# Third convolution part by seven products, the first head's scores ahead of z, and a shorter norm chain, in a hybrid encoder block

## The chip, the cores and the metric

The kernel runs on one core of a Trainium2 chip. The metric is the device time in microseconds (us) of one execution. The engines are named as in the profile: PE multiplies matrices (PEld loads its weights beside it), DVE works on vectors, ACT computes activations, POOL does small operations and issues DMAs through its own queue, SP issues DMAs.

## The reference

One layer over 512 tokens of width 1024, in float32:

```python
h = rmsnorm(x, g_mix)
xc, gb, gc, q, k, v, g_sw, gate_a, gate_r = split(h @ w_in)   # widths 1024 x5, 2048 x2, 1024 x2
u = gc * xc
conv = centred 3-tap convolution of u along the tokens
y_a = (gb * conv) @ w_a_out
ret = retention(rotary(q), rotary(k), v), forward with and backward without the diagonal; 4 heads
ret = per-head normalisation of ret, times g_ret
y_r = (ret * silu(g_sw)) @ w_r_out
x = x + (sigmoid(gate_a) * y_a + sigmoid(gate_r) * y_r) @ w_o
x = x + (silu(rmsnorm(x, g_ffn) @ w_ff_gate) * (rmsnorm(x, g_ffn) @ w_ff_up)) @ w_ff_down   # 2816 wide
return rmsnorm(x, g_final)
```

## The kernel before

**Precision.** Each operand is split in two, a rounded high part (`hi`, a cast on ACT, L203) and the rest (`lo`, a subtract on DVE, L204), and each product is three matmuls: high by high, high by low, low by high (`mm3`, L342 to L344, and the inner loops of `prod`, L383, and `prod_tm`, L427).

**Seven products for eight.** Most large products are done on a grid of 2 x 2 blocks with seven block products, by the Strassen-Winograd scheme. For that, sums of weight quarters are needed (`FORMS`: b11, t1, t2, b21, t3, t4, b22) and sums of activations (`s1` to `s4`). A sum of weights is made in one of two ways: on DVE from two loaded quarters (L301), or, for the sets listed in `SUMMED`, in DRAM by DMAs that add (`sum_step`), so that the kernel loads it ready-made. `strassen` (tokens on the partitions) and `fm_quad` (features on the partitions) run the seven products.

**Order of the weights.** `PLAN` lists every weight unit in the order of use; `take` hands out the next and starts casting and splitting those after it, and `load_raws` and `prefetch_block` issue their loads on SP's queue. There are ten raw tiles (512 KB each) and five pairs of split tiles. A list scheduler at compile time orders the instructions of each engine: the order of the program is the priority, and work that it expects to be ready earlier may go ahead. `tc.issue_after(ins)` puts what the block issues on the engine of `ins` behind it.

**Stages.** First q and k of three heads, then six weight sets of seven products each for v with the swish gate and for the two branch gates (`do_quad`). Their results go to DRAM by POOL's queue (`store`). Behind some of these stores stands a `sum_step`, at up to three places of each `do_quad`; they make the sums for the first two feed-forward sets.

Then the convolution branch. Its 1024 features go in four parts of 256. x and C of parts 0 and 1 are two sets of seven products and B of both is one more (`mix_quads`); their results are split and stored as forms of z (`z_forms`, 16 stores on POOL for both). Then follow head 0's loads, its scores (`do_scores`) and the splitting of its v (`split_v`). Part 2 goes through `do_mix(2)`, with eight block products each for x, C and B (`feature_major`, a block of 48 matmuls). Then for each head: loads of the next head's q, k, v and gate, the value product (`do_pv`), the next head's scores, a transpose (`do_t`), and either part 3 of the convolution (`do_mix(3)`) or the output product of the head before.

After the merge comes the product with `w_o`. While its last products run, each block of 128 tokens (`nb`) is normed for the feed-forward: `join` adds the product to x, `complete` stores it, squares it with a running sum (L1031), adds the two halves' sums (L1035, on ACT), raises to the power -1/2 on POOL (L1036) and scales both halves on DVE (L1039); `tr_o` transposes the result on PE (L1053), splits it and copies it. `first_tokens` runs the first feed-forward products between the transposes.

The feed-forward goes in parts of 3, 4 and 4 sets. The down product of a part (`down`) adds its result into a DRAM copy of x (`ydr`) by accumulating DMAs on POOL (`add_y`); the last part reads that copy.

Of the kernel before, what the change touches and what calls it, by code (L numbers as in the profile page):

```python
# [17 lines left out]
P = 128  # L18
D = 1024
# [49 lines left out]


def plan():

# [73 lines left out]

SUMMED = (("f", 0), ("f", 1), ("o",))

# [23 lines left out]
def block_kernel(ctx: ExitStack, tc: tile.TileContext, xw0, xw, xT, xtok, wpack, wquad, cols, decs, rot, g_ffn, g_final, out):  # L172
# [49 lines left out]
    block = [0]  # L222

    made = []
    ready = []
# [6 lines left out]
    def prefetch_block(loads, splits):  # L232
        i = block[0]
        block[0] += 1
        st = [rawtile(), rawtile()]
        units = []
        for c in range(2):
            if loads:
                loads(c)
            nc.sync.dma_start(st[c], wpack[i][:, c * QH:(c + 1) * QH])  # L240
        for c in range(2):
            hi, lo = unit()
            units.append((hi, lo))
            split(st[c], hi, lo)
            if splits:
                splits(c)
        return units
# [14 lines left out]

    steps = {"quads": sums_of(SUMMED[:2]), "heads": sums_of(SUMMED[2:])}

# [14 lines left out]
    loaded = [0]  # L279

    def load_raws(upto):
        while loaded[0] < len(LOADS) and LOADS[loaded[0]][0] <= upto:
            _, quad, name, u, n = LOADS[loaded[0]]
            t = rawtile()
            src = wsum[quad, name, u] if name[0] == "t" else quarter(quad, name, u)
            nc.sync.dma_start(t[:, 0:n], src[:, 0:n])
            raws[quad, name, u] = t
            loaded[0] += 1

# [499 lines left out]
    def z_forms(s, z):  # L789
# [3 lines left out]
        def put(j, t):  # L793
            n = t.shape[1]
            hl = [t512(F32R)[:, 0:256 * n].rearrange("p (f t) -> p f t", f=n) for _ in range(2)]
            split(t, *hl)
            for d, x in zip(zd[j], hl):
                store(d[:, :, s, :], x.bitcast(F32))
        v, w = (t512().rearrange("p (f t) -> p f t", f=2) for _ in range(2))
# [5 lines left out]
        put(2, w)  # L805
        put(3, x2[:, 1:2])

    def do_mix(s):
        us, c = [], bigtile()[:, 0:2, :]
        feature_major(xg, lambda m, ps: us.append(snap(ps)))  # L810
        u = u_tile()

        def ev_c(m, ps):
            nc.vector.tensor_tensor(out=u[:, m, 1:513], in0=ps, in1=us[m], op=ALU.mult)
            conv(m, 2 * s + m, u[:, m], c[:, m])
        feature_major(xg, ev_c)

        def ev_b(m, ps):
            nc.vector.tensor_tensor(out=c[:, m], in0=ps, in1=c[:, m], op=ALU.mult)
        feature_major(xg, ev_b)  # L820
        z_forms(s, c)

    T1, T2 = slice(0, 256), slice(256, 512)

    def halves(t):
        return t.rearrange("p (m t) -> p m t", m=2)

    def mix_quads():

        c = bigtile().rearrange("p (s m) t -> p s m t", s=2)  # L830
        for s in range(2):
            u, got = u_tile(), {}

            def ev21(ps):
                nc.vector.tensor_tensor(out=u[:, :, 257:513], in0=halves(ps), in1=halves(got["c2"]), op=ALU.mult)

            def ev12(t):
                nc.vector.tensor_tensor(out=u[:, :, 1:257], in0=halves(got["x1"]), in1=halves(t), op=ALU.mult)
            fm_quad(xf, lambda t: got.update(x1=t), ev21, lambda t: got.update(c2=t), ev12)
            for m in range(2):  # L840
                conv(m, 2 * s + m, u[:, m], c[:, s, m])
# [7 lines left out]
        for s in range(2):  # L849
            z_forms(s, c[:, s])  # L850


    def load(src, dt=F32):
        t = bigtile(dt)
        nc.sync.dma_start(t if dt == F32 else t.bitcast(F32), src)
        return t

    def load_head(h):
        tab = misctile(896, "tab")
        nc.sync.dma_start(tab, tabs[h])  # L860
        return [load(t, F32R) for t in qkd[h]], tab, load(vd[h]), load(sgd[h])

# [165 lines left out]
    def complete(nb, half, last):  # L1028
# [3 lines left out]
        if not last:  # L1032
            nc.gpsimd.tensor_scalar_add(ac[:, 3:4], ac[:, 0:1], EPS)
            return
        nc.scalar.activation(ac[:, 4:5], ac[:, 1:2], AF.Identity, bias=ac[:, 3:4])  # L1035
        nc.gpsimd.tensor_tensor(out=ac[:, 5:6], in0=ac[:, 4:5], in1=mhalf[:, 0:1], op=ALU.pow)  # L1036
# [65 lines left out]

    def ev(tt):
        if tt == 0:
            tr_o(1)
        join(2 + tt, 0, a[tt])
        complete(2 + tt, 0, 1)
# [5 lines left out]
    act = {}  # L1113
    gates = {}

    def act_tiles(names):
# [6 lines left out]
    def gated(q, th, g, u):  # L1123
# [5 lines left out]
        if not gates.get(q0):  # L1129
# [3 lines left out]
                               for j in range(2))  # L1133
        s = t512()
        nc.scalar.activation(s, g, AF.Silu)
        nc.vector.tensor_tensor(out=s, in0=u, in1=s, op=ALU.mult)
# [71 lines left out]
    def down(n):  # L1208
        strassen(n, act_forms(), lambda tt, t: add_y(t, tt, 0), lambda tt, ps: add_y(snap(ps), 2 + tt, 0),
                 lambda tt, t: add_y(t, 2 + tt, 1), lambda tt, t: add_y(t, tt, 1))  # L1210

# [194 lines left out]
```

## Time and profile before

| | |
|---|---|
| median of three runs | 1022.86 us (1022.56 to 1025.2) |
| profiled execution | 1025.12 us |
| span in that execution, first to last instruction | 1023.3 us |
| mean granted clock of PE | 0.997 |
| busy PE / DVE / ACT / POOL | 1014.1 / 903.1 / 550.0 / 137.0 us |

The times of one execution hang together; the profiled one lies 2.26 us above the median of the others. A row of a timeline reads: start, duration, engine, line, operation, output <- inputs, shape, count, and in brackets the idle time ahead of it and what ended that. A row of the waits reads: engine and line that waited, what it waited for, us in total, times, the longest. SPq, POOLq and ACTq are DMAs issued by that engine.

### The profile page before, as it was taken

What the parts mean: (1) busy time and instruction counts of PE and PEld (TensorE: products, weight loads), DVE (VectorE), ACT (ScalarE), POOL (GpSimd) and SP (SyncE); (2) the same over time, 40 slices, a digit from 0 to 9 for tenths busy, and PEclk for the clock granted to TensorE, in tenths of its full rate; (3) what the DMA queues carried; (4) which work ended last, traced back from release to release, by engine and by line L of the source; (5) the groups of instructions that cost most, each with busy time, mean ns of one, the idle gap of its engine ahead of it and who ended that gap; (6) DMA issues with size and microseconds to landing.
All of it is one profiled execution on the core that took longest, in us unless ns stands there. A gap on an engine that the chain in (4) does not pass through costs nothing.

```text
span 1023.3 us, 14820 instructions
## 1 busy us (share of the span) xinstructions
PE 1014.1 (99%) x5586; PEld 884.6 (86%) x5586; DVE 903.1 (88%) x1161; ACT 550.0 (54%) x748; POOL 137.0 (13%) x225
## 2 busy tenths in 40 slices
PE   9999999999999999999999999999999999999997
PEld 7888888888888998888888888879998999899986
DVE  7877998979798988797989998999998999889996
ACT  7556655553656455343543335586654565556554
POOL 0020221222112003202122100020002000110011
PEclk9999999999999999999999999999999999999999
DMA  9525487694766657848597855473318522663533
GB/s 351 191 86 187 166 297 216 212 315 151 256 204 227 256 198 267 326 146 331 125 342 294 292 181 165 162 268 96 125 41 224 178 84 83 190 161 104 166 68 98
DMA packets 53352, 200.24 MB, mean 196 GB/s; under 512 B 7264, under 2 KB 7392, under 8 KB 48672
## 3 DMA queue, kind: packets, MB, share of 16 engines
q1 hardware_dynamic: 37600, 137.39, 38.8%
q0 software_dynamic: 15392, 61.62, 20.7%
q8 instruction: 44, 0.72, 0.3%
q10 hardware_dynamic: 288, 0.29, 0.1%
q14 instruction: 28, 0.23, 0.1%
HBM read 160.73 MB, written 55.31 MB: 211 GB/s over the span
## 4 chain that ended last, share of the span: by engine, by line
PE 93%; DVE 4%; issue 1%; ACT 1%; DMA 0%; POOL 0%; POOLq 0%; DVEq 0%; ACTq 0%
PE bank L427 35%; PE bank L383 28%; PE bank L342 10%; PE bank L344 10%; PE bank L343 10%; DVE wlo L204 1%; DVE xform L204 1%; DVE big L1026 1%; PE bank L477 0%; DMA ydr<-big 0%; DVE big L1006 0%; PE bank L662 0%; DVE big L980 0%; PE bank L1053 0%; DVE big L979 0%
## 5 line engine op out<-in xcount | busy, mean ns | idle before, releaser
L203 ACT CAST whi<-raw 128x1024 fp32r<-128x1024 f32 (+2 forms) x299 | 303.1, 1028 | 268.4 <-PE bank L427 64.7
L204 DVE TENSOR_TENSOR wlo<-raw,whi 128x1024 fp32r<-128x1024 f32 (+2 forms) x300 | 353.1, 1193 | 70.6 <-ACT whi L203 70.1
L383 PE MATMUL bank<-xform,whi 128*128 128x256 f32 x1424 | 258.8, 284 | 0.0
L383 PEld LDWEIGHTS bank<-xform,whi 128*128 128x128 f32 x1424 | 223.4, 193 | 0.9 <-ACT t L434 0.5
L383 PE MATMUL bank<-xform,wlo 128*128 128x256 f32 x712 | 201.6, 284 | 0.0
L427 PE MATMUL bank<-whi,big 128*128 128x512 f32 x596 | 187.6, 390 | 0.0
L427 PE MATMUL bank<-whi,xform 128*128 128x512 f32 x496 | 157.1, 390 | 0.0
L301 DVE TENSOR_TENSOR raw<-raw 128x1024 f32<-128x1024 f32 (+1 forms) x128 | 151.8, 1204 | 3.6 <-DMA raw<-wquad 2.7
L383 PEld LDWEIGHTS bank<-xform,wlo 128*128 128x128 f32 x712 | 137.1, 193 | 0.0
L427 PEld LDWEIGHTS bank<-whi,big 128*128 128x128 f32 x596 | 111.8, 188 | 24.2 <-ACT t L434 0.4
L427 PE MATMUL bank<-wlo,big 128*128 128x512 f32 x298 | 116.0, 389 | 0.0
L427 PEld LDWEIGHTS bank<-whi,xform 128*128 128x128 f32 x496 | 93.0, 188 | 19.6 <-DVE xform L204 0.4
L427 PE MATMUL bank<-wlo,xform 128*128 128x512 f32 x248 | 96.5, 389 | 0.0
L434 ACT COPY t<-bank 128x512 f32<-128x512 f32 x105 | 61.2, 586 | 56.0 <-PE bank L383 29.7
L342 PE MATMUL bank<-big,whi 128*128 128x512 f32 x220 | 85.7, 390 | 0.0
L344 PE MATMUL bank<-big,wlo 128*128 128x512 f32 x220 | 85.6, 389 | 0.0
L343 PE MATMUL bank<-big,whi 128*128 128x512 f32 x220 | 85.6, 389 | 0.0
L427 PEld LDWEIGHTS bank<-wlo,big 128*128 128x128 f32 x298 | 56.0, 188 | 11.4
L427 PEld LDWEIGHTS bank<-wlo,xform 128*128 128x128 f32 x248 | 46.6, 188 | 9.5
L342 PE MATMUL bank<-whi,big 128*128 128x512 f32 x128 | 49.8, 389 | 0.0
L343 PE MATMUL bank<-wlo,big 128*128 128x512 f32 x128 | 49.8, 389 | 0.0
L344 PE MATMUL bank<-whi,big 128*128 128x512 f32 x128 | 49.8, 389 | 0.0
(200 smaller groups left out, 1372.5 us busy)
## 6 DMA issues: line engine op xcount, KB each, us to landing
raw<-wquad SPq DMA_DIRECT2D x140, 512.0 KB, 4.6
raw<-wpack SPq DMA_DIRECT2D x42, 512.0 KB, 5.8
t_f<-wquad POOLq DMA_DIRECT2D x12, 512.0 KB, 6.9
z<-t POOLq DMA_DIRECT2D x24, 256.0 KB, 4.6
t_o<-wquad POOLq DMA_DIRECT2D x12, 512.0 KB, 6.9
zform<-z POOLq DMA_DIRECT2D x6, 1024.0 KB, 7.7
v<-t POOLq DMA_DIRECT2D x16, 256.0 KB, 5.2
sg<-t POOLq DMA_DIRECT2D x16, 256.0 KB, 4.8
```

Source lines behind the costliest of these rows:

```text
L203: first = (round or nc.scalar.copy)(hi, src)
L204: low_of[0] = nc.vector.tensor_tensor(out=lo, in0=src, in1=hi.bitcast(F32), op=ALU.subtract)
L301: nc.vector.tensor_tensor(out=t, in0=t, in1=raws[quad, more, u][:, 0:n], op=ALU.add)
L342: nc.tensor.matmul(ps, lh, rh, start=first, stop=False)
L343: nc.tensor.matmul(ps, lh, rl, start=False, stop=False)
L344: nc.tensor.matmul(ps, ll, rh, start=False, stop=last)
L383: nc.tensor.matmul(o, l[:, c], r[:, k], start=start and s == 0 and k == 0 and i == 0, stop=stop and k == 3 and i == 2, skip_group_check=True)
L427: nc.tensor.matmul(pss[tt], l, r[:, c], start=start and k == 0 and i == 0, stop=stop and k == n - 1 and i == 2, skip_group_check=True)
L434: nc.scalar.copy(t, ps)
L1026: nc.vector.tensor_tensor(out=yt, in0=yt, in1=ps, op=op)
```

## The change

Four things are changed.

1. **Third part.** x and C of part 2 of the convolution become a set of seven products (`XC`), behind those of parts 0 and 1 and ahead of B of parts 0 and 1. Its weight sums are made in DRAM: it stands first in `SUMMED`, and `do_quad` gets one more place for a `sum_step` (four for three). `do_mix(2)` keeps B alone.
2. **Order.** Head 0's q, k, v and gate are loaded among the weight loads of the second and third sets. Its v is split and its scores run ahead of `z_forms` of parts 0 and 1 (`put_z`). Head 1's q and k are loaded on POOL's queue behind the last store of z. Weight blocks that follow are loaded on SP behind head 0's loads.
3. **Norm.** The add of the two sums (L1035) goes from ACT to POOL, and for token block 2 the `join` stands ahead of `tr_o(1)`.
4. **First down part.** It is stored to a tensor of its own (`first`) by plain DMAs. Eight accumulating DMAs from DRAM to DRAM add it to `ydr`, behind a small POOL operation that reads the gate of the first set of the second part.

```diff
+XC = ("x", C_XC + 512, C_GC + 512)
-    for c0, c1 in ((C_XC, C_GC), (C_XC + 256, C_GC + 256), (C_GB, C_GB + 256)):
+    for c0, c1 in ((C_XC, C_GC), (C_XC + 256, C_GC + 256), XC[1:], (C_GB, C_GB + 256)):
...
-        for c in (C_XC, C_GC, C_GB):
+        for c in (C_GB,) if s == 2 else (C_XC, C_GC, C_GB):
...
-SUMMED = (("f", 0), ("f", 1), ("o",))
+SUMMED = (XC, ("f", 0), ("f", 1), ("o",))
...
-            nc.sync.dma_start(st[c], wpack[i][:, c * QH:(c + 1) * QH])
+            with tc.issue_after(behind[-1].ins) if behind else nullcontext():
+                nc.sync.dma_start(st[c], wpack[i][:, c * QH:(c + 1) * QH])
...
-    steps = {"quads": sums_of(SUMMED[:2]), "heads": sums_of(SUMMED[2:])}
+    steps = {"quads": sums_of(SUMMED[:1]) + sums_of(SUMMED[1:3]), "heads": sums_of(SUMMED[3:])}
...
+            if among and loaded[0] % 3 == 0:
+                with tc.issue_after(raw.ins):
+                    among.pop(0)()
...
-                if tt and not o:
+                if tt:
                     sum_step(last)
...
+    def xc_quad(s, c):
+        u, got = u_tile(), {}
+        def ev21(ps):
+            nc.vector.tensor_tensor(out=u[:, :, 257:513], in0=halves(ps), in1=halves(got["c2"]), op=ALU.mult)
+        def ev12(t):
+            nc.vector.tensor_tensor(out=u[:, :, 1:257], in0=halves(got["x1"]), in1=halves(t), op=ALU.mult)
+        fm_quad(xf, lambda t: got.update(x1=t), ev21, lambda t: got.update(c2=t), ev12)
+        for m in range(2):
+            conv(m, 2 * s + m, u[:, m], c[:, m])
+    def put_z():
+        for s in range(2):
+            stored = z_forms(s, made_z[0][:, s])
+        with tc.issue_after(stored.ins):
+            second.extend(load(t, F32R, nc.gpsimd) for t in qkd[1])
...
+        xc_quad(0, c[:, 0])
+        head = []
+        for src, dt in ((qkd[0][0], F32R), (qkd[0][1], F32R), (vd[0], F32), (sgd[0], F32)):
+            among.append(lambda src=src, dt=dt: head.append(load(src, dt)))
+        xc_quad(1, c[:, 1])
+        part2.append(bigtile()[:, 0:2, :])
+        xc_quad(2, part2[0])
...
-        for s in range(2):
-            z_forms(s, c[:, s])
+        while among:
+            among.pop(0)()
+        tab = misctile(896, "tab")
+        nc.sync.dma_start(tab, tabs[0])
+        made_z.append(c)
+        behind.append(last[3])
+        return head[0:2], tab, *head[2:]
...
     def do_mix(s):
+        if s == 2:
+            c = part2[0]
+        else:
             ... x and C by two blocks, as before
...
-    mix_quads()
-    nxt = load_head(0)
+    nxt = mix_quads()
+    vv, sg = split_v(nxt[2]), nxt[3]
     p = do_scores(nxt[0], nxt[1])
-    vv, sg = split_v(nxt[2]), nxt[3]
+    put_z()
     do_mix(2)
...
-            nxt = load_head(h + 1)
+            nxt = load_head(h + 1, second if h == 0 else None)
...
-        nc.scalar.activation(ac[:, 4:5], ac[:, 1:2], AF.Identity, bias=ac[:, 3:4])
+        nc.gpsimd.tensor_tensor(out=ac[:, 4:5], in0=ac[:, 1:2], in1=ac[:, 3:4], op=ALU.add)
...
+        join(2 + tt, 0, a[tt])
         if tt == 0:
             tr_o(1)
-        join(2 + tt, 0, a[tt])
         complete(2 + tt, 0, 1)
...
+    first = dram.tile([S, D], F32, name="first_part")
+    def put_first(t, nb, half):
+        nc.gpsimd.dma_start(first[nb * P:(nb + 1) * P, half * 512:(half + 1) * 512], t)
+    def add_first(behind):
+        with tc.issue_after(behind.ins):
+            for nb in range(NB):
+                for half in range(2):
+                    add_y(first[nb * P:(nb + 1) * P, half * 512:(half + 1) * 512], nb, half)
...
             pair(q)
+            if q == q_add:
+                mark = small.tile([P, 1], F32, tag="mark", name="mark", bufs=1)
+                add_first(nc.gpsimd.tensor_scalar_add(mark, gate_of[0][:, 0:1], 0.0))
         if q0 + n < NQ:
-            down(n)
+            down(n, add_y if q0 else put_first)
```

More of the change, by code (lines that the diff above doesn't have):

```diff
@@ L1 @@
-from contextlib import ExitStack
+from contextlib import ExitStack, nullcontext
 import numpy as np
@@ L222, in block_kernel @@
     block = [0]
+    behind = []
     made = []
@@ L279, in block_kernel @@
     loaded = [0]
+    among = []
     def load_raws(upto):
@@ L797, in put @@
             for d, x in zip(zd[j], hl):
-                store(d[:, :, s, :], x.bitcast(F32))
+                stored = store(d[:, :, s, :], x.bitcast(F32))
+            return stored
         v, w = (t512().rearrange("p (f t) -> p f t", f=2) for _ in range(2))
@@ L805, in z_forms @@
         put(2, w)
[L806 to L821, printed above, removed]
+        return put(3, x2[:, 1:2])
     T1, T2 = slice(0, 256), slice(256, 512)
@@ L826, in halves @@
         return t.rearrange("p (m t) -> p m t", m=2)
+    def xc_quad(s, c):
[7 more added lines that the diff above has]
+            conv(m, 2 * s + m, u[:, m], c[:, m])
+    part2, second, made_z = [], [], []
+    def put_z():
[3 more added lines that the diff above has]
+            second.extend(load(t, F32R, nc.gpsimd) for t in qkd[1])
     def mix_quads():
         c = bigtile().rearrange("p (s m) t -> p s m t", s=2)
-        for s in range(2):
[L832 to L841, printed above, removed]
+        xc_quad(0, c[:, 0])
[5 more added lines that the diff above has]
+        xc_quad(2, part2[0])
         def times(s, t):
@@ L848, in mix_quads, with do_mix, ev_c, ev_b @@
         fm_quad(xf, times(0, T1), times(0, T2), times(1, T2), times(1, T1))
-        for s in range(2):
-            z_forms(s, c[:, s])
-    def load(src, dt=F32):
+        while among:
[5 more added lines that the diff above has]
+        return head[0:2], tab, *head[2:]
+    def do_mix(s):
+        if s == 2:
+            c = part2[0]
+        else:
+            us, c = [], bigtile()[:, 0:2, :]
+            feature_major(xg, lambda m, ps: us.append(snap(ps)))
+            u = u_tile()
+            def ev_c(m, ps):
+                nc.vector.tensor_tensor(out=u[:, m, 1:513], in0=ps, in1=us[m], op=ALU.mult)
+                conv(m, 2 * s + m, u[:, m], c[:, m])
+            feature_major(xg, ev_c)
+        def ev_b(m, ps):
+            nc.vector.tensor_tensor(out=c[:, m], in0=ps, in1=c[:, m], op=ALU.mult)
+        feature_major(xg, ev_b)
+        z_forms(s, c)
+    last = []
+    def load(src, dt=F32, queue=nc.sync):
         t = bigtile(dt)
-        nc.sync.dma_start(t if dt == F32 else t.bitcast(F32), src)
+        last.append(queue.dma_start(t if dt == F32 else t.bitcast(F32), src))
         return t
-    def load_head(h):
+    def load_head(h, qk=None):
         tab = misctile(896, "tab")
         nc.sync.dma_start(tab, tabs[h])
-        return [load(t, F32R) for t in qkd[h]], tab, load(vd[h]), load(sgd[h])
+        return qk or [load(t, F32R) for t in qkd[h]], tab, load(vd[h]), load(sgd[h])
     def do_scores(qk, tab):
@@ L1134, in gated @@
         s = t512()
+        gate_of[0] = s
         nc.scalar.activation(s, g, AF.Silu)
@@ L1198, in pair, with down @@
         gated(q, 0, st["p1"], u2)
+    first = dram.tile([S, D], F32, name="first_part")
     def add_y(t, nb, half):
         nc.gpsimd.dma_start(out=ydr[nb * P:(nb + 1) * P, half * 512:(half + 1) * 512], in_=t, accum_op=ALU.add)
+    def put_first(t, nb, half):
[5 more added lines that the diff above has]
+                    add_y(first[nb * P:(nb + 1) * P, half * 512:(half + 1) * 512], nb, half)
     def act_forms():
         return {name: of(t) for name, t in act.items()}
-    def down(n):
-        strassen(n, act_forms(), lambda tt, t: add_y(t, tt, 0), lambda tt, ps: add_y(snap(ps), 2 + tt, 0),
-                 lambda tt, t: add_y(t, 2 + tt, 1), lambda tt, t: add_y(t, tt, 1))
+    def down(n, add):
+        strassen(n, act_forms(), lambda tt, t: add(t, tt, 0), lambda tt, ps: add(snap(ps), 2 + tt, 0),
+                 lambda tt, t: add(t, 2 + tt, 1), lambda tt, t: add(t, tt, 1))
     first_tokens(*FIRST_PRODUCTS[0])
```

3 lines of the change are left out of this document (2 added, 1 removed).

## The prediction

> **What bounds the kernel.** I read the page first, then PE's waits, then stretches of the span cut at changes of PE's work, and last the instructions around PE's only mid-span pause.
>
> ```profile
> span 1023.3 us, 14820 instructions
> PE 1014.1 (99%) x5586; PEld 884.6 (86%) x5586; DVE 903.1 (88%) x1161; ACT 550.0 (54%) x748; POOL 137.0 (13%) x225
> PE 93%; DVE 4%; issue 1%; ACT 1%; DMA 0%; POOL 0%; POOLq 0%; DVEq 0%; ACTq 0%
> ```
> ```profile
> PE bank L1053 <- DVE t L1039: 1.6, 1, 1.6
> PE bank L477 <- DVE t L474: 1.4, 1, 1.4
> ```
>
> PE is busy for 1014.1 of 1023.3 us and the chain that ended last is 93% PE. In the whole span PE waits for another engine twice: 1.4 us at the start, which nothing here touches, and 1.6 us for the second norm (L1039 feeds the transposes of L1053). So there are only two ways to save: fewer columns for PE to stream, or that one wait. Everything else in this change moves work that is hidden now; it can lose time and hardly gain any. The time to start from: the profiled execution took 1025.12 us around its span of 1023.3. The median of the runs shown is 1022.86, lower by 2.26, and I come back to that gap.
>
> **Part 1, the third part by seven products.** The two parts of the convolution that already use seven products, and the third part that does not, give both prices:
>
> ```profile
> 323.23:343.61 20.38, 20.38 (x170) 20.22 (x169) 18.44 (x23) 10.63 (x15) 2.69 (x5) 1.00 0.78 275
> 343.61:363.99 20.38, 20.38 (x171) 20.21 (x170) 18.42 (x20) 8.57 (x12) 0.00 (x0) 1.00 0.62 238
> 389.80:411.56 21.76, 21.76 (x97) 18.02 (x96) 17.40 (x26) 10.36 (x16) 7.25 (x12) 1.00 0.73 249
> 411.56:422.44 10.88, 10.88 (x49) 9.01 (x48) 5.32 (x8) 2.70 (x3) 0.00 (x0) 1.00 1.00 418
> 422.44:433.32 10.88, 10.88 (x49) 9.01 (x48) 10.10 (x22) 4.30 (x7) 6.88 (x11) 1.00 0.83 286
> ```
>
> The columns are the stretch, its length, the busy time of PE, PEld, DVE, ACT and POOL, then clock, DMA share and GB/s. Rows 1 and 2 are one set of seven products each: 7 x 24 matmuls of 256 columns. Row 3 is what the third part's x and C cost now: 2 blocks x 2 x 8 x 3 = 96 matmuls of 512 columns. The edit takes 21.76 out and puts 20.38 in: **-1.38 us** on PE, which has no gap in any of these rows. It isn't the full eighth that seven for eight promises, since a 256-column matmul costs 20.38 / 168 = 121 ns against 21.76 / 96 = 227 ns, more than half.
>
> The cover for this saving is DVE: 18.4 busy of 20.38 in a set whose four sums are made on DVE. The new set takes ready sums from DRAM and leaves out four adds of this group:
>
> ```profile
> L301 DVE TENSOR_TENSOR raw<-raw 128x1024 f32<-128x1024 f32 x124 | 149.2, 1220 | 0.9
> t_f<-wquad POOLq DMA_DIRECT2D x12, 512.0 KB, 6.9
> ```
>
> So about 18.4 - 4 x 1.2 = 13.6 of 20.38: DVE keeps up. Behind it, the single block that stays (row 4) leaves DVE half idle. The price of the ready sums: eight more 512 KB sums in DRAM, and seven loads of 512 KB on SP where four were. The sums are queued on POOL behind the stores of the six earlier weight sets, one store more per set giving the slots, and each step of this single chain needs the one before. Those slots are one product apart, 24 matmuls of 227 ns = 5.4 us, while a sum's first step lands in 6.9, so POOL may stand about 1.5 us at three or four steps, with the stores of v and the swish gate queued behind it and, behind those, their tiles. PE sees that only if tiles run out for its snaps. I take 0; the bounds are 0 and 1.5 for one slip that reaches PE. One more unused quarter (b12 of the new set) is loaded near the end: 0, as PE does not wait there.
>
> **Part 2, the norm's chain.** The pause and what led to it:
>
> ```profile
> 676.53 1.03 PE L1053 MATMUL bank<-ident,t 128*128 128x128 f32 x8
> 677.32 0.48 PE L427 MATMUL bank<-whi,xform 128*128 128x512 f32 x1
> ...
> 680.98 0.21 POOL L1033 TENSOR_SCALAR ac<-ac 128x1 f32<-128x1 f32 x1 [1.36 <-ACT t L1031]
> ...
> 682.39 1.28 DVE L204 TENSOR_TENSOR xform<-bank,xform 128x512 fp32r<-128x512 f32 x2
> 682.71 1.08 ACT L203 CAST whi<-raw 128x1024 fp32r<-128x1024 f32 x1
> 683.59 1.27 DVE L1026 TENSOR_TENSOR big<-big,bank 128x512 f32<-128x512 f32 x2
> 683.66 1.10 ACT L1059 COPY big<-bank 128x512 f32<-128x512 f32 x2
> 684.61 0.68 ACT L1031 ACTIVATE t<-big 128x512 f32<-128x512 f32 x1
> 684.78 2.35 DVE L204 TENSOR_TENSOR wlo<-raw,whi 128x1024 fp32r<-128x1024 f32 x2
> 685.14 0.24 ACT L1031 ACTIVATION_READ_ACCUMULATOR t<-big 128x1 f32 x1
> 685.24 1.08 ACT L203 CAST whi<-raw 128x1024 fp32r<-128x1024 f32 x1
> 686.17 0.33 ACT L1035 ACTIVATE ac<-ac 128x1 f32<-128x1 f32 x1
> 686.51 0.28 PE L383 MATMUL bank<-xform,wlo 128*128 128x256 f32 x1
> 686.59 0.97 POOL L1036 TENSOR_TENSOR ac<-ac,mhalf 128x1 f32<-128x1 f32 x1 [5.39 <-ACT ac L1035]
> 687.59 1.41 DVE L1039 SCALAR_TENSOR_TENSOR t<-big,ac,gb 128x512 f32<-128x512 f32 x2 [0.46 <-POOL ac L1036]
> 688.40 1.71 PE L1053 MATMUL bank<-ident,t 128*128 128x128 f32 x8 [1.61 <-DVE t L1039]
> 694.01 1.03 PE L1053 MATMUL bank<-ident,t 128*128 128x128 f32 x8
> ```
>
> PE is through at 686.51 + 0.28 = 686.79 and starts the transposes at 688.40, 0.81 after L1039 began. The chain back: pow on POOL (L1036), the add on ACT (L1035), which stood behind a weight cast from 685.38 (the square's accumulator read) to 686.17, the square (L1031), the join (L1026). The edit does two things to it. The join goes ahead of the two 128x512 subtracts of tr_o(1), so from 683.59 to about 682.4; but the square needs ACT, which is in a cast until 683.8 and then owes two copies, so it gains 0.3 to 0.9, not 1.2. And the add goes to POOL: from the read's end to pow was 686.59 - 685.38 = 1.21; by way of POOL it is a hop and a 128x1 add (0.21 in the row of L1033), some 0.3 to 0.7, so 0.5 to 0.9 less. Together L1039 could start 0.8 to 1.8 earlier. Then DVE decides: its two weight subtracts run to 687.13. If L1039 stays behind both, it gains 0.46; if it gets between them, up to 1.5. I take **-0.9** off the pause of 1.61; the ends are 0 and -1.61.
>
> The pause has a second price:
>
> ```profile
> 686.00:688.00 2.00, 0.79 (x7) 0.59 (x5) 1.54 (x2) 1.79 (x4) 0.97 (x1) 1.00 0.86 234
> 688.00:690.00 2.00, 1.50 (x9) 1.30 (x10) 2.00 (x3) 1.16 (x4) 0.05 (x1) 0.83 0.95 352
> 690.00:692.00 2.00, 2.00 (x11) 2.00 (x11) 1.56 (x4) 1.07 (x2) 0.55 (x1) 0.50 0.33 133
> 692.00:694.00 2.00, 2.00 (x16) 2.00 (x15) 1.20 (x2) 0.59 (x1) 0.00 (x0) 0.82 0.01 4
> ```
>
> The granted clock (third column from the end) goes to half from about 689.3 to 692.4. From 688.40 to 694.01 PE did 8 transposes (0.79, 676.53 to 677.32) and one product (24 x 0.12 = 2.88): 3.67 us of work in 5.61, so the half clock cost **1.94**. In this execution it follows the pause; with a pause of 0.7 it should not come. Against the profiled execution the sum is 1025.12 - 1.38 - 0.9 - 1.94 = 1020.9. The 2.26 between that execution and the median is close to 1.94, so I take it that the median runs pause without the dip: 1022.86 - 1.38 - 0.9 = **1020.6**, which I forecast.
>
> The Trainium skill ("TensorE: Matmul & The Clock Gate", Part 1) says that the clock is halved only after an idle window of about 3.4 us, in a window that runs free of the kernel. The length fits, about 3.1 us in the rows; the pause doesn't, as 1.61 us was enough here. If that rule held, the dip would not be this pause's and would stay: 1025.12 - 1.38 - 0.9 = 1022.8 in an execution that has it.
>
> **Part 3, scores ahead of z, second head's q and k on POOL.** Each queue it passes:
>
> ```profile
> 380.83 0.72 POOL L633 DMA_DIRECT2D z<-t  x1 [52.06 <-ACT t L203]
> ...
> 395.95 2.55 POOL L633 DMA_DIRECT2D z<-t  x4 [0.37 <-ACT t L203]
> 396.54 1.88 DVE L873 SCALAR_TENSOR_TENSOR t<-bank,tab 128x512 f32<-128x512 f32 x3
> ```
> ```profile
> big<-qh SPq DMA_DIRECT2D x1, 1024.0 KB, 8.6
> big<-ql SPq DMA_DIRECT2D x1, 1024.0 KB, 10.6
> DMA to landing us min/median/max: 5.4/7.4/9.4
> ```
>
> The 16 z stores ran from 380.83 to 398.50, 8.7 us past the last score matmul (389.80), with the scores' evictions behind them on DVE from 396.54. Turned round, the evictions come first: 4 x (L873 + its subtract) at 0.6 each = 4.9, so the last z store goes out about 13.6 past the scores. Only then does POOL issue the second head's q and k. Issuing takes about 1.2 and they land after 7.4 (the third row, 1 MB loads on POOL's queue) to 10.6: in at 22.2 to 25.4. PE wants them after the B block and the first value product (rows 4 and 5 of the stretches): 21.76 past the scores. On paper that is 0.4 to 3.5 late. Against it: z's work can begin inside the B products as it does now (380.83 lies before their end), the set before them leaves DVE 4.8 us freer, and the planner can put the fourth part's x block, 10.88 of ready work, ahead. I take 0 and keep 3.5, plus 1.94 if a dip follows. The first head's four loads go among the weight loads on SP at a DMA share of 0.62; 0, for PE reaches those scores 20 us later than now. The fourth part's weight loads queue behind them: 0, with five weight tiles in hand.
>
> **Part 4, first down part's plain stores.** Eight accumulating stores become plain ones and eight DRAM-to-DRAM accumulations of 256 KB follow on POOL's queue behind the first gate of the second part. PE has no wait in that region, so no gain; I take 0, with the 1.5 of a queue slip as the other end.
>
> **Rivals.** (a) The runs compared have the dip before and not after: 1022.86 - 1.38 - 0.9 - 1.94 = 1018.6, and 1017.9 if the whole pause goes. For it: the profiled execution had the dip. Against: the 2.26 by which the median lies lower; and for the whole pause, DVE's two subtracts. (b) L1039 stays last on DVE: the norm yields under 0.46, giving 1021.3. (c) The dip isn't the pause's, and stays: 1022.8 at most. (d) The other side: the second head's q and k come late. It decides when PE's pause there passes about 3.4 us and brings a dip: 3.5 + 1.94 - 1.38 - 0.9 = +3.2, 1026.0. For it stands the count above; against it the planner's freedom.
>
> **Numbers.** 0.3% is 3.07 us, about what a measurement tells. Forecast 0.42 (its own range 1019.6 to 1021.9), (a) 0.31, (b) 0.07, (c) 0.07, (d) and other new waits 0.13. (a) and a twentieth from the forecast's low edge lie beyond -3.07: faster 0.36. (d) lies beyond the other bound for the most part: slower 0.12. The rest, 0.52, is no change. The range is 1018.0, most of (a), to 1024.6, where the shorter waits of (d) end.
>
> **What would show it.** Part 1: 168 matmuls of L383 more and 96 of 512 columns fewer, the B block straight after the scores, and no PE wait between 323 and 405. Part 2: the wait of L1053 for L1039 below 1 us, clock 1.00 in every slice from 680 to 700, and L1035's row on POOL. Part 3: no wait of PE for a load of q or k near 432. Wrong, if a PE wait stands in that place, if DVE falls behind so that PE waits for a weight subtract, or if the pause is as long as before.

## The result and the profile after

The changed kernel took 1031.41 us (median of six runs, 1030.23 to 1032.88), the kernel before 1024.09 on the same chip (six runs): ratio 1.0073, interval 1.006 to 1.0086. The forecast was 1020.6. The change loses 7.3 us where I expected a gain of 2.3, and lies outside the range. The six times of the kernel before are three of 1022.56 to 1022.98 and three of 1025.2 to 1025.54 (the profiled one, with the half clock behind the norm's pause, took 1025.12), so that its median of 1024.09 lies between two groups.

The page of the changed kernel, the two lines at the top and the chain:

```profile
span 1028.5 us, 14992 instructions
PE 1014.5 (99%) x5658; PEld 886.9 (86%) x5658; DVE 907.2 (88%) x1167; ACT 552.8 (54%) x748; POOL 156.1 (15%) x248
PE 84%; issue 10%; DMA 2%; POOL 2%; DVE 2%; ACT 1%; POOLq 0%; DVEq 0%; ACTq 0%
```

PE was 93% of the chain and is 84%; DMA and POOL, both under half a per cent before, have 2% each, and "issue" went from 1% to 10%. PE's busy time hardly moved (1014.1 before) although the new set streams less, for matmuls under a halved clock count longer. PE's waits in the changed kernel:

```profile
PE bank L354 <- DMA big<-qh: 4.9, 1, 4.9
PE bank L489 <- DVE t L486: 1.4, 1, 1.4
PE bank L1096 <- DVE t L1082: 0.5, 1, 0.5
PE bank L355 <- DMA big<-ql: 0.3, 1, 0.3
```

The norm's wait fell from 1.6 to 0.5 (L1039 is L1082 here), and a wait for the second head's q (`qh`, `ql` are head 1's two loads) has appeared: 4.9 + 0.3. The place, in stretches of two microseconds with the columns of the earlier stretches, and PE's instructions around it:

```profile
432.00:434.00 2.00, 0.00 (x0) 0.00 (x0) 1.74 (x5) 0.23 (x1) 0.69 (x1) 1.00 0.99 418
434.00:436.00 2.00, 0.00 (x0) 0.00 (x0) 2.00 (x6) 0.00 (x0) 0.00 (x0) 0.95 1.06 446
436.00:438.00 2.00, 1.23 (x3) 1.03 (x4) 1.14 (x4) 0.00 (x0) 0.56 (x1) 0.50 0.97 397
438.00:440.00 2.00, 1.69 (x4) 0.88 (x4) 0.00 (x0) 0.00 (x0) 0.00 (x0) 0.50 0.99 381
440.00:442.00 2.00, 2.00 (x6) 1.52 (x6) 0.00 (x0) 0.00 (x0) 1.79 (x4) 0.50 1.04 414
442.00:444.00 2.00, 2.00 (x9) 1.62 (x8) 1.10 (x2) 1.10 (x2) 2.00 (x5) 0.84 0.72 279
```
```profile
431.45 0.39 PE L356 MATMUL bank<-big 128*128 128x512 f32 x1
436.77 2.08 PE L354 MATMUL bank<-big 128*128 128x512 f32 x4 [4.94 <-DMA big<-qh]
```

PE stops at 431.84, resumes at 436.77, and the clock is at half from about 435.8 to 442.6. So 4.94 + 0.31 of waiting and 442.6 - 436.8 = 5.8 us at half speed, worth about 2.9: some 8.2 at this one place. Against that stand -1.38 from the seven products and -1.1 - 1.94 from the norm (its pause, and the dip behind it, which is gone). The sum, 8.2 - 4.4 = +3.8, is 1.3 short of the +5.1 between the two profiled executions (1030.23 and 1025.12). The larger part of that lies in the norm, which gave 2.2 and not 3.0 (worked out under Part 2 below). Against the three runs before without the dip, 1022.8 on average, there is none to save: the sum is 8.2 - 2.5 = +5.7, and +8.6 was measured. The profiled execution is the fastest of the changed kernel's six, 1.2 below their median. The other five have lower mean clocks (0.993 to 0.995 against 0.996), so more time at half clock, but where it lay no trace shows.

What made q late, on POOL and on SP, and the loads' landing in the same stretch (count, size, median us from issue to landing):

```profile
409.73 0.74 POOL L645 DMA_DIRECT2D z<-t  x1 [80.50 <-ACT t L207]
412.23 0.70 POOL L645 DMA_DIRECT2D z<-t  x1 [1.76 <-DVE t L208]
414.77 6.01 POOL L645 DMA_DIRECT2D z<-t  x9 [1.84 <-ACT t L207]
421.36 3.22 POOL L645 DMA_DIRECT2D z<-t  x5 [0.58 <-DVE t L208]
424.65 0.55 POOL L898 DMA_DIRECT2D big<-qh  x1
425.19 0.54 POOL L898 DMA_DIRECT2D big<-ql  x1
```
```profile
423.75 0.59 SPq L898 DMA_DIRECT2D big<-v  x1
424.50 1.16 SPq L898 DMA_DIRECT2D big<-sg  x1
```
```profile
big<-v SPq DMA_DIRECT2D x1, 1024.0 KB, 10.5
big<-sg SPq DMA_DIRECT2D x1, 1024.0 KB, 14.7
big<-qh POOLq DMA_DIRECT2D x1, 1024.0 KB, 12.1
big<-ql POOLq DMA_DIRECT2D x1, 1024.0 KB, 14.3
```

The scores end at 409.92. The first z store goes out at 409.73, the sixteenth ends at 424.58, 14.7 past the scores; only then come the two loads, and they take 12.1 and 14.3 us. The same head's v and gate are issued on SP within 1.5 us of them and share the DMA engines (DMA share 0.97 to 1.06 in the stretches above, up to 442). In the kernel before the same four loads stood on SP alone, q and k first, issued from 406.54 to 408.16. Its q and k took the 8.6 and 10.6 that the prediction shows; the two behind them:

```profile
big<-v SPq DMA_DIRECT2D x1, 1024.0 KB, 12.7
big<-sg SPq DMA_DIRECT2D x1, 1024.0 KB, 14.4
```

So four such loads took about as long before. What the change lost, besides the late issue, is that q and k go first.

### The profile page after: what moved, and what is told of

It reads as the page before. It is cut to its first block, busy times and chain, and to the rows that moved or that the text cites. A ratio compares the mean times of both kernels' runs of the same rounds, so it can differ in the third digit from the quotient of the medians.

```text
span 1028.5 us, 14992 instructions
## 1 busy us (share of the span) xinstructions
PE 1014.5 (99%) x5658; PEld 886.9 (86%) x5658; DVE 907.2 (88%) x1167; ACT 552.8 (54%) x748; POOL 156.1 (15%) x248
## 4 chain that ended last, share of the span: by engine, by line
PE 84%; issue 10%; DMA 2%; POOL 2%; DVE 2%; ACT 1%; POOLq 0%; DVEq 0%; ACTq 0%
PE bank L439 37%; PE bank L395 21%; PE bank L355 8%; PE bank L356 8%; PE bank L354 8%; DMA big<-ql 1%; POOL z L645 1%; DMA raw<-wquad 1%; DVE raw L313 0%; PE bank L489 0%; DVE wlo L208 0%; PE bank L1096 0%; PE bank L1041 0%; ACT whi L207 0%; PE bank L674 0%
## 5 line engine op out<-in xcount | busy, mean ns | idle before, releaser
L207 ACT CAST whi<-raw 128x1024 fp32r<-128x1024 f32 (+2 forms) x302 | 306.6, 1029 | 268.0 <-PE bank L439 64.6
L395 PE MATMUL bank<-xform,whi 128*128 128x256 f32 x1488 | 269.9, 284 | 0.1
L395 PEld LDWEIGHTS bank<-xform,whi 128*128 128x128 f32 x1488 | 232.3, 192 | 1.8 <-ACT t L446 0.9
L395 PE MATMUL bank<-xform,wlo 128*128 128x256 f32 x744 | 209.8, 283 | 0.0
L439 PE MATMUL bank<-whi,big 128*128 128x512 f32 x596 | 187.0, 389 | 0.0
L395 PEld LDWEIGHTS bank<-xform,wlo 128*128 128x128 f32 x744 | 142.5, 192 | 0.0
L354 PE MATMUL bank<-big,whi 128*128 128x512 f32 x188 | 73.5, 391 | 0.0
L356 PE MATMUL bank<-big,wlo 128*128 128x512 f32 x188 | 73.2, 389 | 0.0
L355 PE MATMUL bank<-big,whi 128*128 128x512 f32 x188 | 73.1, 389 | 0.0
L207 ACT CAST big<-t 128x512 fp32r<-128x512 f32 (+1 forms) x60 | 34.5, 580 | 35.4 <-DVE t L916 17.9
L354 PE MATMUL bank<-whi,big 128*128 128x512 f32 x128 | 49.8, 389 | 0.0
```

Of the source, the lines that this page charges most:

```text
L207: first = (round or nc.scalar.copy)(hi, src)
L354: nc.tensor.matmul(ps, lh, rh, start=first, stop=False)
L355: nc.tensor.matmul(ps, lh, rl, start=False, stop=False)
L356: nc.tensor.matmul(ps, ll, rh, start=False, stop=last)
L395: nc.tensor.matmul(o, l[:, c], r[:, k], start=start and s == 0 and k == 0 and i == 0, stop=stop and k == 3 and i == 2, skip_group_check=True)
L439: nc.tensor.matmul(pss[tt], l, r[:, c], start=start and k == 0 and i == 0, stop=stop and k == n - 1 and i == 2, skip_group_check=True)
```

## Experiments

**Head 1's q and k elsewhere.** Three versions of the changed kernel. `qk_sp` loads them on SP as before the change:

```diff
-        with tc.issue_after(stored.ins):
-            second.extend(load(t, F32R, nc.gpsimd) for t in qkd[1])
...
-            nxt = load_head(h + 1, second if h == 0 else None)
+            nxt = load_head(h + 1)
```

> The changed kernel with one thing undone: head 1's q and k are loaded on SP with its v and gate, as before, and not on POOL behind z's stores. Theory (late loads): PE's wait of 4.94 + 0.31 us for q and k goes, and the half clock behind it (8.3 us in all by the spacing of the matmuls from 430 to 445), so some 1031.4 - 8.3 = 1023, at or just under the kernel before. Rival (overload: DVE and POOL fall behind in the whole passage because of the third set and the new order): PE still waits near 432, for a score eviction or a weight subtract, and the time stays above 1027.

Measured 1027.22 (six runs, 1024.77 to 1028.6), 1.0038 of the kernel before (1.0025 to 1.0052): 4.2 us less than the whole change. The wait for q is gone, but the time is not at the 1023 that the theory gave. Its profiled execution, shown below, is the fastest of the six, 2.4 below their median.

`qk_pool_ahead_z` leaves them on POOL's queue, but ahead of z's stores:

```diff
+        second.extend(load(t, F32R, nc.gpsimd) for t in qkd[1])
         for s in range(2):
             stored = z_forms(s, made_z[0][:, s])
-        with tc.issue_after(stored.ins):
-            second.extend(load(t, F32R, nc.gpsimd) for t in qkd[1])
```

> The changed kernel with q and k of head 1 still on POOL, but ahead of z's 16 stores in its queue. Theory (late because of the place behind z): issued near 410 for 424.65, landed by 422, 10 us ahead of PE's need at 431.7; no wait, about 1023, within 1 us of the version with q and k on SP. Rival (POOL's queue is slow for 1 MB loads, wherever they stand): landing still takes 12 to 14 us, which would hide here too, but the z stores shift by some us; then v's split or z would show a wait.

1027.56, ratio 1.0037 (1.0024 to 1.0051), with no wait for q; there the two loads landed after 8.2 and 9.6 us. Hence it is the place behind sixteen stores that costs, not POOL's queue as such.

`v_later` keeps q and k where the change puts them and loads head 1's v and gate later, on POOL behind the first value product:

```diff
-            nxt = load_head(h + 1, second if h == 0 else None)
+            tab = misctile(896, "tab")
+            nc.sync.dma_start(tab, tabs[1])
...
+            with tc.issue_after(power.ins):
+                nxt = (second, tab, load(vd[1], F32, nc.gpsimd), load(sgd[1], F32, nc.gpsimd))
```

> The changed kernel with q and k left behind z on POOL, but head 1's v and gate loaded after the first value product on POOL's queue, so that they don't share the DMA engines with q and k. If sharing is the larger part (landing 12.1 and 14.3 us for 8.6 and 10.6): q and k land 8 to 9 us after 424.65, at 433 to 434, PE waits 1 to 2 us for 5.2, and the time is 1025 to 1028. If the late issue is nearly all: the wait stays above 4 us and the time above 1030.

1032.79, ratio 1.0087 (1.0072 to 1.0101). PE's waits:

```profile
PE bank L354 <- ACT big L979: 2.6, 1, 2.6
PE bank L355 <- DMA big<-ql: 2.0, 1, 2.0
PE bank L354 <- DMA big<-qh: 1.8, 1, 1.8
```

The two loads now land after 8.9 and 11.8 us, and the wait for q and k went from 5.2 to 3.8. So the shared DMA engines are part of the lateness and the late issue the larger part. As a repair it fails: a wait of 2.6 comes at 515.9, and the clock is at half twice, from 436.8 to 443.7 and from 518.7 to 522.2.

**What is left in `qk_sp`.** PE's waits of `qk_sp`, and the instructions behind the first of them on PE, ACT and DVE:

```profile
PE bank L354 <- ACT big L976: 1.7, 1, 1.7
PE bank L395 <- ACT whi L207: 0.8, 1, 0.8
```
```profile
481.31 0.43 DVE L208 TENSOR_TENSOR t<-big,t 128x256 fp32r<-128x256 f32 x1 [4.05 <-DMA z<-t]
506.39 2.56 ACT L210 ACTIVATE big<-big,cols_sb 128x512 fp32r<-128x512 f32 x4 [8.45 <-DVE big L222]
508.86 2.03 ACT L976 COPY big<-bank 128x512 f32<-128x512 f32 x4
509.48 0.50 PE L354 MATMUL bank<-big 128*128 128x512 f32 x1 [1.74 <-ACT big L976]
```

The same chain in the kernel before:

```profile
480.17 0.43 DVE L204 TENSOR_TENSOR t<-big,t 128x256 fp32r<-128x256 f32 x1 [2.53 <-DMA z<-t]
507.72 2.02 ACT L935 COPY big<-bank 128x512 f32<-128x512 f32 x4
509.48 0.39 PE L342 MATMUL bank<-big 128*128 128x512 f32 x1
```

`z_forms` splits into ten working tiles of 512 columns and the pool has nine. The split that needs the tenth waits until a store of z has landed and freed a tile, and DVE stands in the meantime: 2.53 us before, 4.05 here. Everything behind it on DVE is later, the transposes (L222) too, then ACT's scaled splits (L210) and, behind them, the copies (L976) that free PE's banks. In the kernel before those copies start at 507.72 and PE comes at 509.48; here they start at 508.86, and PE, which is ready at 507.74, has to wait. Why is the stall longer? The stores of z land 9.7 us after issue in that stretch (6.3 before). SP's loads for head 2 come 4 us later and now lie on top of them, which is a likely reason, though no run moves these loads alone. The row of the first of them, `qk_sp` and then before:

```profile
472.37 0.36 SPq L896 DMA_DIRECT2D big<-v  x1
```
```profile
468.65 0.33 SPq L855 DMA_DIRECT2D big<-v  x1
```

Two theories: the order (scores ahead of z) makes DVE late; or the eight block products that were taken out were where DVE caught up. `sp_eight` is `qk_sp` with the third part by eight block products again (the set's sums in DRAM go with it, the order stays):

```diff
-    for c0, c1 in (..., XC[1:], (C_GB, C_GB + 256)):
+    for c0, c1 in (..., (C_GB, C_GB + 256)):
-        for c in (C_GB,) if s == 2 else (C_XC, C_GC, C_GB):
+        for c in (C_XC, C_GC, C_GB):
-        part2.append(bigtile()[:, 0:2, :])
-        xc_quad(2, part2[0])
...
```

> The changed kernel with head 1's q and k on SP and with the third part's x and C by eight block products again (its set of seven and their sums in DRAM left out); order, norm and down stores as changed. Theory (without the 21.8 us of block products behind the scores DVE is 4 us behind): DVE catches up in those block products as before, no PE wait near 508, and the time is within 1 us of before. Rival (the loss lies in the order itself or in the down stores): the time stays at 1026 to 1028.

`sp_inplace` is `qk_sp` with the last low part of z written over its source, so that nine tiles are enough:

```diff
-            hl = [t512(F32R)... for _ in range(2)]
+            hl = [t512(F32R)... for _ in range(1 if j == 3 else 2)]
+            if j == 3:
+                hl.append(t.bitcast(F32R))
             split(t, *hl)
```

> The changed kernel with head 1's q and k on SP, and z's last low part written in place, so that z_forms needs nine working tiles and not ten of the nine there are. Theory (DVE stands 4.05 us at 477 for a working tile that a z store still holds, and PE's wait near 508 comes from that): DVE's wait for a z store goes, PE's wait near 508 goes or falls under 0.5, and the time falls by 1.5 to 3 us against the version with q and k on SP, to 1024 to 1026. Rival (DVE's general lag): the wait near 508 stays at 1.5 us or more.

`sp_eight` took 1023.75, ratio 0.9998 (0.999 to 1.0007): no loss is left, and DVE's stall at that place is back at 2.46. So the order alone is not to blame; the set of seven in place of the block products is. Whether by the time that the block products gave DVE or by the set's own sums and loads, `sp_eight` can't tell, since it undoes all of it. `sp_inplace` took 1023.29, ratio 0.9997 (0.9989 to 1.0006), with the seven products kept: one working tile fewer is worth 3.9 us of `qk_sp`'s median. (The kept trace of `qk_sp`, its fastest execution, shows only 1.7 of that as a wait.) The wait near 508 is absent from its profile; the longest of PE's waits in it is another:

```profile
PE bank L395 <- ACT whi L207: 1.5, 1, 1.5
```

`before_inplace` is the control, that edit alone in the kernel before:

> Control: the kernel before with z's last low part written in place and nothing else. Theory: in the kernel before DVE's wait of 2.5 us for a z store ends before PE needs anything from it, so the time is within 0.5 us of before, and what this edit gave the version with q and k on SP (3.9 us) is the price of that wait once PE is earlier. Rival (the edit is a gain of its own): 1 us or more below before.

Ratio 1.0004 (0.9995 to 1.0014). Its median is 1025.29, as six of its eleven runs have the mean clock of 0.997 of runs with the dip; the other five, 1022.65 to 1023.51, are as fast as the kernel before without it. The tile isn't worth anything by itself; it only mends what the set of seven did.

**Each part by itself, in the kernel before.** `xc_only` adds the third set of seven products (and its summed weights) and leaves the order as it was:

```diff
-SUMMED = (("f", 0), ("f", 1), ("o",))
+SUMMED = (XC, ("f", 0), ("f", 1), ("o",))
...
-        for s in range(2):
+        for s in range(3):
             u, got = u_tile(), {}
```

> The kernel before with part 1 alone: the third set of seven products with its sums in DRAM; loads of heads, the order of scores and z, the norm and the down stores as before. Theory (the saving is real on PE but is given back at the first value product of head 2, which stands on a DVE chain with little slack): PE is 1.4 us earlier until 470 and waits 0.5 to 2 us near 508; the time is 1023 to 1025.5. Rival (the loss that is left is from the new order): no wait of PE after 405 and 1.4 us less than before, 1021.7.

1031.61, ratio 1.0076 (1.0063 to 1.009), as slow as the whole change and far above the 1025.5 that the theory allowed. PE's longest waits, and the two rows that end them:

```profile
PE bank L345 <- ACT big L206: 3.5, 1, 3.5
PE bank L346 <- DVE big L207: 3.5, 1, 3.5
```
```profile
424.49 1.04 ACT L206 CAST big<-big 128x1024 fp32r<-128x1024 f32 x1
428.32 1.22 DVE L207 TENSOR_TENSOR big<-big 128x1024 fp32r<-128x1024 f32 x1
```

With z ahead of the scores' evictions, the first value product waits 7 us for the split of v, which stands behind z and the scores; in the kernel before 21.76 us of block products lie between. DVE again stands for z's stores, for up to 2.78 us at a time, and the clock is at half from 426.3 to 433.2. The change's new order answers this, and its own placing of q and k brings back a wait of about the same size.

`norm_only` has both edits of the norm, `pool_add_only` only the add on POOL:

```diff
-        nc.scalar.activation(ac[:, 4:5], ac[:, 1:2], AF.Identity, bias=ac[:, 3:4])
+        nc.gpsimd.tensor_tensor(out=ac[:, 4:5], in0=ac[:, 1:2], in1=ac[:, 3:4], op=ALU.add)
```

> The kernel before with the norm's two edits alone (the add on POOL, the join ahead of the transposes of block 1). Theory: PE's pause at the third norm block falls from 1.61 to about 0.5 as in the changed kernel, and with it goes the half clock (1.94) in the runs that have it: 1.1 to 3 us less than before, 1021.0 to 1023. Rival: the time is within 0.5 us of before, and the gain of the changed kernel there is due to other weights' order.

> The kernel before with the norm's add on POOL alone, the join where it was. By the prediction's steps this gives 0.5 to 0.9 of the pause (1.61) and the moved join 0.3 to 0.9 more, as DVE allows. Theory: the add on POOL is what lets the scaling go between DVE's two weight subtracts, so the pause is at 0.5 to 0.8 here too. Rival: both are needed, and the pause stays above 1.1. The time is within 1 us of before in both cases.

1023.71, ratio 1.0007 (0.9997 to 1.0016), and 1023.81, ratio 1.0001 (0.9992 to 1.001). Neither time fell, where 1.1 to 3 less was forecast for `norm_only`. In both the pause is 0.5 (was 1.6), so the add does it all and the join's new place nothing measurable. Waits of `norm_only`, the add in it, and then in `pool_add_only`:

```profile
PE bank L383 <- ACT whi L203: 0.7, 1, 0.7
PE bank L1053 <- DVE t L1039: 0.5, 1, 0.5
```
```profile
684.42 0.90 POOL L1035 TENSOR_TENSOR ac<-ac 128x1 f32<-128x1 f32 x1 [4.63 <-ACT t L1031]
```
```profile
685.03 0.41 POOL L1035 TENSOR_TENSOR ac<-ac 128x1 f32<-128x1 f32 x1 [5.12 <-ACT t L1031]
```

With the join moved the add starts 0.61 earlier, but takes 0.90 for 0.41, and pow starts at 685.39 for 685.52. These 0.13 are no gain, since PE reaches the pause 0.13 earlier too (686.27 for 686.40). And what the norm saves returns a hundred microseconds later: PE then reaches a weight cast (whi) before it is done, since DVE's weight sum ahead of it waits for its load. Of `norm_only`:

```profile
780.35 2.36 DVE L301 TENSOR_TENSOR raw<-raw 128x1024 f32<-128x1024 f32 x2 [1.18 <-DMA raw<-wquad]
```

`first_only` has the first down part's plain stores and the later accumulation:

```diff
-            down(n)
+            down(n, add_y if q0 else put_first)
...
+            if q == q_add:
+                add_first(nc.gpsimd.tensor_scalar_add(mark, gate_of[0][:, 0:1], 0.0))
```

> The kernel before with the first down part's plain stores and the eight later additions alone. Theory: no PE wait of before lies there, so within 0.5 us of before; the cast that PE waits for near 787 in the versions where PE is earlier doesn't show. Rival (the 2 MB that the additions move hold up weight loads): a PE wait for a weight cast between 785 and 810 and 1 to 3 us more.

1023.1, ratio 0.9999 (0.999 to 1.0007): no difference.

**Can the last wait be taken away?** Two versions of `sp_inplace` look for what makes the weight cast late: one leaves out the first down part's stores and their addition, the other cuts the DVE sums of that part's weights to eight columns.

```diff
-            if q == q_add:
+            if False:
...
-                down(n, add_y if q0 else put_first)
+                down(n, add_y if q0 else (lambda t, nb, half: None))
```

> The best version so far (q and k on SP, z's last low part in place) with the first down part's result left out: neither stored nor added to x. It asks where PE's wait of 1.5 us for a weight cast near 787 comes from. If the stores' traffic holds up the weight loads: the wait goes and the time falls by about 1.5 us, to 1021.8. If the weights are late because of DVE and the raw tiles it frees: the wait stays at 1 us or more.

```diff
+            w = 8 if quad == ("d", 0) else n
-            nc.vector.tensor_tensor(out=t, in0=t, in1=raws[quad, more, u][:, 0:n], op=ALU.add)
+            nc.vector.tensor_tensor(out=t[:, 0:w], in0=t[:, 0:w], in1=raws[quad, more, u][:, 0:w], op=ALU.add)
```

> The best version so far with the eight weight sums on DVE of the first down part cut to 8 columns each, so their products are of wrong weights; loads, tiles and PE's work are the same. It takes some 9 us of DVE's work out between 750 and 785. If DVE sets when the weights near 787 are ready: PE's wait there goes and the time falls by 1.5 us, to 1021.8 or lower. If the DMAs do: the wait stays at 1 us or more.

1023.09, ratio 0.999 (0.998 to 0.9999), and 1022.82, ratio 0.9987 (0.9978 to 0.9996), not the 1021.8 of either theory. The wait for the cast is absent from both profiles. But both come to that place 2.0 to 2.5 us later than `sp_inplace`, more than the 1.5 that it waited there, so it isn't shown which of the two makes the cast late. For the wait near 508 is there again, 1.3 in both; the row of the first:

```profile
PE bank L354 <- ACT big L978: 1.3, 1, 1.3
```

Up to 740 us these two and `sp_inplace` have the same instructions in the same order on each of PE, DVE, ACT and POOL; so that wait comes and goes from one execution to the next. The traces show by what. Written in place, z's last low part lies in one of the large tiles, and ACT begins to split head 2's v into such tiles within 0.15 us of the landing of that store, in all three (the profile names no releaser, so this is read from the times). In `sp_inplace` the store goes out at 477.43, with its landing time and ACT's row:

```profile
z<-big POOLq DMA_DIRECT2D x1, 128.0 KB, 9.6
487.09 1.05 ACT L207 CAST big<-big 128x1024 fp32r<-128x1024 f32 x1 [3.63 <-issue]
```

In the other two the store landed after 11.0 and 10.9 us and ACT began at 489.48 and 489.01; in `before_inplace` it landed after 5.6, and no wait is listed. So the edit moves the wait from a working tile to a large one, and PE waits when the store lands late: the working tile mends most of it, not all.

The ratios are taken against all runs of the kernel before, and ten of those 33 (eight of 29 for `sp_inplace`) have the mean clock of 0.997 of runs with the dip. Against the other runs before, `sp_inplace` is 0.3 us slower on average (1023.34 against 1022.99), and the two versions here are 0.3 and 0.4 faster. No version with the whole result beat the kernel before by more than the measurement can tell.

## Why the prediction was wrong, step by step

**Part 1, the saving: right, the cover: wrong.** The third set on PE, of the changed kernel:

```profile
363.57:383.95 20.38, 20.38 (x170) 20.16 (x169) 17.45 (x20) 10.12 (x12) 0.00 (x0) 1.00 0.51 172
```

20.38 as forecast, without a gap, and PE waits for nothing from 323 to 430. DVE was to be busy for 13.6 and is for 17.45: other work moved in, and it keeps up in this stretch. What the step left out is that the removed 21.76 us were cover. In that stretch DVE was busy 17.40, and in the next 10.88 only 5.32: spare time in which the splits of z, the scores and v caught up. The trace of `xc_only` shows this at the first value product; for the wait near 508 it is argued. I asked whether DVE keeps up inside the new set, not what it had been doing beside the old one. With the 1.38 saved taken off, `xc_only` prices that at 8.5 us (1031.61 against 1023.08) with the old order, `qk_sp` at about 4 with the new one. The sums in DRAM, put at 0 to 1.5, cost PE nothing in the changed kernel; the longest wait of PE for a weight subtract among these versions is 0.4, near 160 in `xc_only`.

**Part 2: the pause right in size, the gain not.** The pause went from 1.61 to 0.53, -1.1 against -0.9 forecast, and L1039 did get between DVE's two weight subtracts. My split was not: the add on POOL does it alone. The clock, of the changed kernel:

```profile
692.00:694.00 2.00, 1.49 (x13) 1.28 (x11) 1.26 (x3) 2.00 (x4) 1.49 (x3) 1.00 1.01 378
```

1.00 in every slice from 688 to 702, so rival (c) isn't the case in this execution (two of the eleven runs of `norm_only` do have a mean clock of 0.997; no trace shows where). But a shorter pause is not yet time. The 500 matmuls that run from 646.81 to 726.59 in the kernel before take 79.78 us there, 78.23 in `before_inplace`, where the same pause has no dip behind it, and 77.53 to 77.55 in `norm_only`, `pool_add_only` and the changed kernel. So the dip cost 1.5, for 1.94 in the prediction, and the norm's edits save 0.7, for 0.9: of the 1.1 that the pause lost, 0.4 returns in steps too short to be listed as waits. What the step missed is that the rest returns too: from 726 to PE's last matmul `norm_only` takes 291.2 us, the wait for the cast at 787 included, and `before_inplace` 290.2.

The assumption that before's median runs have no dip holds for the larger groups (8 of 29 runs seem to have it, at about 1025.0 to 1025.8 and a mean clock of 0.997, the others take 1022.4 to 1023.9 at 0.998 or 0.999). Of the six that the change was measured against three took 1025.2 or more, so rival (a) had half of its condition; its low time failed with Part 3.

**Part 3, "I take 0": the step that failed.** The need was forecast right (21.76 past the scores; PE came at 431.84, 21.92 past). The last z store was put at 13.6 past and came at 14.7. The landing was bounded by 10.6 from rows in which q and k were the first of four loads on one queue; it was 12.1 and 14.3. (The other bound, 7.4, comes from a row that mixes loads of 512 KB with those of 1 MB, whose median is 7.7.) I had counted 0.4 to 3.5 late (3.6 by the sum itself), then set the count aside for "the planner's freedom": z's work would begin inside the B products. It didn't, and the first store of z goes out at 409.73, as the scores end, DVE being busy for 19.30 of the 20.60 us from 404.0 to 424.6:

```profile
404.00:424.60 20.60, 20.60 (x101) 17.42 (x100) 19.30 (x35) 10.04 (x16) 10.64 (x16) 1.00 0.63 203
```

And I listed the queues that were passed, but not what would be issued on the other queue at the same time: v and the gate. So rival (d) was the case, with a wait of 4.9 for 3.5 and a half clock worth 2.9 for 1.94. It had the right mechanism, its count was done, and it got 0.13.

**Part 4: right** for the edit alone, no difference.

The largest error is thus one of weight: the sum of the numbers said "late", and an argument without a number said "not late". The second loss, by the working tile, was in none of the rivals. In the medians the two are of about the same size: 4.2 from the changed kernel to `qk_sp`, 3.9 from there to `sp_inplace`.

## What to carry to other kernels

When work is taken off the engine that bounds, ask first what the other engines catch up on in that time; an engine with 5 us to spare in each of two stretches may need them for what comes after. A load that is queued behind stores is as late as the last of them, and its landing time must be read beside whatever another queue issues then. Count the working tiles that a helper needs at once: with one too few, an engine stands until a store lands, and every delay of the stores becomes a delay of that engine. If the store is made to hold another tile instead, ask who needs that one next.

## What the runs showed of the hardware

After the pause of 4.94 us the granted clock was at half for 6.83 us (435.80 to 442.63), and for 3.41 (689.30 to 692.72) after the pause of 1.61 us in the kernel before; the prediction read 3.1 from slices of 2 us. The first clock record of each trace, full clock, stands at 5.73 and 6.64, and the half clock begins 430.08 and 682.67 us after it: 126 and 200 steps of 3.413 us. `xc_only` (419.84, 123 steps) and `v_later` (430.08 and 512.00, 126 and 150 steps) fit the same grid, and each of their dips lasts one step or two. The Trainium skill ("TensorE: Matmul & The Clock Gate", Part 1) has the clock judged in free-running windows of about 3.4 us, and these traces agree. It gives an idle window as what halves the clock; in the profiled execution of the kernel before a pause of 1.61 us, under half a window, was enough. Why it was not in others, as in those of `first_only` and `before_inplace` (pause 1.6, mean clock 0.999), no run here shows.

Four loads of 1 MB issued within 2 us landed after 8.6 to 14.4 us, in the order of issue, when all stood on SP's queue, and after 10.5 to 14.7 us when they were spread over two queues. And a 128x1 add on POOL took 0.41 us in one place and 0.90 in another, where I had reckoned with 0.21.
